# Sample cross-attention with stationary queries in quarter tiles, and state space parameters worked out during the input projection

## The chip, the cores and the metric

The kernel runs on one core of one Trainium2 chip. The metric is device time in microseconds (us) of one execution, from launch to end, as the median of several runs. The core has five engines with queues of their own: TensorE (PE, with its weight loads listed apart as PEld), VectorE (DVE), ScalarE (ACT), GpSimd (POOL) and SyncE (SP, which only issues transfers). An engine takes its instructions strictly in the order of its queue; engines wait for each other by semaphores.

## What is computed

One inference step of one decoder layer, for a prompt of 1024 tokens and, with the same weights, for 64 sample tokens (8 sequences of 8 tokens with a paged cache of 8192 past tokens each). Cut to the parts that the change touches:

```python
z = rmsnorm(x, norm_mix_pre) @ w_in          # one projection: 1024 -> 1056 columns
c_q, c_kv, k_r, u = split(z)                 # 256 | 256 | 32 | 512
attn_out = mla_mixer(c_q, c_kv, k_r, ...)    # samples: attention over the paged cache
# state space mixer: 32 groups x 16 channels, 64 states
dt  = exp(ssm_log_dt); mag = exp(dt * a_re)
abr, abi = mag * cos(dt * a_im), mag * sin(dt * a_im)
...                                          # powers of (abr, abi), input and output tables, scan, GLU
# cross-attention of 4 heads x 128 into 256 memory tokens; for the samples mk, mv are caches per sequence
q  = (h @ w_q_mem).reshape(b, l, 4, 128)
s  = einsum('bqhd,bmhd->bhqm', q, mk) * MEM_SCALE
pr = softmax(s)
o  = einsum('bhqm,bmhd->bqhd', pr, mv).reshape(b, l, 512) @ w_o_mem
# then a gated MLP of 2816 columns
```

## The kernel before, in words

The layer is a chain of stages. In the profiled execution they lie as follows: projection 0 to 129 us (`stage_in`), paged sample attention with everything that is put beside it 129 to about 700 (`stage_par`), prompt attention to 873, mixing to 991, cross-attention to 1204 (`stage_mem`), the MLP to the end.

**Projection.** Nine tiles of tokens: the 64 samples first (numbered 8), then prompt tiles t = 0 to 7. Each takes 72 matmuls of up to 512 columns into three PSUM banks `z` (L488), split into high and low halves for three-product accuracy: ACT makes `xh` from `xT`, DVE `xl` (L325, L326), one tile ahead. A tile's `z` is read out by ACT (`cz`) and by DVE (`kr_raw` L496, two copies into `u_all` L498 and L499). At t == 2 `dec_start` prepares the sample queries of the paged attention: they go through DRAM, `qld` and then `Qb` in four transfers of 512 KB on SP, and POOL issues the gathers of the first cache pages `kf` and `rf`.

**The parallel stage.** `gen_dec` walks the cache: DVE transposes each gathered block (`kT<-kf`, L1033, eight blocks of 1.2 us, and one of `rf`), PE makes scores S (L1044), DVE their maxima (`mx`, L1065), ACT exponentials, PE transposes and values (`ov`, L1109). Beside it a generator `side()` runs `gen_ssm`, `gen_glu`, `gen_memkv`, `gen_q` and `gen_attw`. The instructions of both are recorded and put into a new order by a class `Order` (list scheduling by costs, for PE, DVE, ACT and POOL); SP's transfers keep their place by the recorded order and priorities. `gen_ssm` begins with a parameter part: it loads `prm` (L617), computes two exponentials by polynomials on DVE (L634 to L645), phases with a Sin table on ACT (L669, L670), powers `pw` by squaring on DVE and POOL, factors `f` and tables `cs`. It also brings the sample inputs `u_sn` as `us8`, 8 partitions, in 8 transfers (L623), and turns them by 32 PE transposes of 8x8 blocks (L736) into `Us`. Then come tables and chunks per state group (`BB`, `W1T`, `W`, scan `Z`).

**Cross-attention.** `stage_mem` runs prompt tiles t = 0 to 7 of 128 tokens: query transposes, `project(t - 1)` (output projection, L1736), scores and softmax (L335 to L337, L1751 to L1758), the next tile's query projection `query_z`, transposes of the probabilities `Pm` (L1839) and values (L1850). The sample work is put among the tiles by a hand-written list `sample[t]`. Scores: `sample_k(b)` keeps the keys of a sequence stationary (128x128 per head and half of the memory) and moves the 8 query columns (L1777), 8 matmuls for each of 8 sequences, t = 1 to 4. At t = 5 `sample_w` and `sample_pT` transpose all scores (64 rows x 4 heads), make the softmax, and transpose back. Values: `sample_v(b)` keeps V stationary and moves 8 columns of the transposed probabilities (L1809), t = 5 and 6. `sample_o` is the output projection of the samples at t = 7. PSUM: six banks `b` for the prompt, one bank `sbank` and one bank `smp` for the samples. Each f32 matmul is two passes in the trace, so L1777 and L1809 have 128 passes each; a transpose is one.

Of the kernel before, what the change touches and what calls it, by code (L numbers as in the profile page):

```python
# [9 lines left out]
F32 = mybir.dt.float32  # L10
# [3 lines left out]
AF = mybir.ActivationFunctionType  # L14
OP = mybir.AluOpType
AX = mybir.AxisListType
# [282 lines left out]
class Kern:  # L299
# [96 lines left out]
    def stage_in(self):  # L396
# [82 lines left out]
        for n, t in enumerate(order):  # L479
# [40 lines left out]
            if t == 1:  # L520

                qctx = ExitStack()
                qp = self.pool("q_s", 1, qctx, side="right")
                w = self.q_weights(qp, qp)
                self.q_s = pers.tile([64, 768], F32, tag="qy", name="q_s")
                self.query_rows(qp, [zp.tile([128, 512], F32, tag="z", name="z") for _ in range(2)], self.q_s,
                                self.cqTh_s, self.cqTl_s, *w, self.csS[:, 0], self.csS[:, 1])
                qctx.close()
            if t == 2:
                self.dec_start(lambda: zp.tile([128, 512], F32, tag="z", name="z"))  # L530
# [72 lines left out]
    def gen_ssm(self):  # L603
# [44 lines left out]
        exp(w["dt"][:, None, :], ldt[:, None, :], 1)  # L648
        ex = new(c2, "ex", [128, 2, 32])
# [3 lines left out]
        exp(mags, ex, 2)  # L653
        rho8 = new(c1, "rho8", [128, 32])
# [17 lines left out]
        V.tensor_scalar(ph[:, 0], s2, -2.0, 1.0, op0=OP.mult, op1=OP.add)  # L672

# [7 lines left out]
        for n in (1, 2, 4):  # L681
            bc = lambda a: a[:, None, :].to_broadcast([128, n, 32])
            self.cmul([pw[:, k, n + 1:2 * n + 1] for k in (0, 1)], [pw[:, k, 1:n + 1] for k in (0, 1)],
                      [bc(pw[:, k, n]) for k in (0, 1)], [t[:, :n] for t in tmp], V, G)
        pwr = pw[:, :, 7::-1]
# [17 lines left out]
        V.tensor_scalar_mul(f[:, 3], w["t2"], -1.0)  # L703

# [23 lines left out]
        ssd = new(c1, "ssd", [16, 32])  # L728
        nc.sync.dma_start(ssd, i["ssm_d"])

        pp = self.pool("sp", 2, ctx, space=PSUM)
        psum = lambda: pp.tile([128, 512], F32, tag="ps", name="ps")
        Us = new(c1, "Us", [128, 32, 8])
        ps = psum()[:, 0:256].rearrange("p (g b) -> p g b", b=8)
        for g in range(32):
            nc.tensor.transpose(ps[:, g], us8[:, g].rearrange("p j c -> p (j c)"), self.ident[:8, :8])  # L736
        nc.scalar.activation(Us, ps, AF.Copy)
        tctx.close()
# [945 lines left out]
    def stage_mem(self):  # L1684
# [17 lines left out]
        kv = lambda: sp.tile([128, 2, 512], F32, tag="kv", name="kv")  # L1702
# [57 lines left out]

        smp = {}

        def sample_q(q):
            ps = sbank()
            for h in range(4):
                nc.tensor.transpose(ps[:, h, :64], q[:, h * 128:(h + 1) * 128], self.ident[:64, :64])
            smp["qT"] = sp.tile([128, 4, 64], F32, tag="qTs", name="qTs", bufs=1)
            V.tensor_copy(smp["qT"], ps[:, :, :64])
            smp["st"] = ps_.tile([128, 2, 4, 64], F32, tag="smp", name="smp")

        def sample_k(b):
            qT, st = smp["qT"], smp["st"]
            kT = flat(kv()).rearrange("p (h k m) -> p h k m", h=4, k=2)
            nc.sync.dma_start(kT.rearrange("p h k m -> p (h k m)"), i["mem_kT"][b])
            for k in range(2):
# [4 lines left out]
        def sample_w():  # L1780
            sT = sp.tile([128, 2, 4, 64], F32, tag="sT", name="sT", bufs=1)
            V.tensor_copy(sT, smp["st"])
            ps = sbank()
            s4 = ps.rearrange("p (a k) m -> p a (k m)", a=2)
            for a in range(2):
                for k in range(2):
                    nc.tensor.transpose(ps[:, a * 2 + k], sT[:, k, 2 * a:2 * a + 2].rearrange("p h t -> p (h t)"),
                                        self.ident)
            Pm = smp["P"] = sp.tile([128, 2, 256], F32, tag="Pms", name="Pms", bufs=1)
            l = sp.tile([128, 4], F32, tag="l8", name="l8")  # L1790
            softmax(s4, 2, Pm, l, 0, "mx8")

        def sample_pT():
            Pm = smp["P"]
            ps = sbank()
            for a in range(2):
                for k in range(2):
                    nc.tensor.transpose(ps[:, k * 2 + a], Pm[:, a, k * 128:(k + 1) * 128], self.ident)
            smp["pT"] = sp.tile([128, 2, 4, 64], F32, tag="sT", name="pTs", bufs=1)
            V.tensor_copy(smp["pT"].rearrange("p k h t -> p (k h t)"), flat(ps))  # L1800
            smp["po"] = ps_.tile([128, 2, 4, 64], F32, tag="smp", name="smp")[:, 0]

        def sample_v(b):
            pT, po = smp["pT"], smp["po"]
            vb = kv()
            nc.sync.dma_start(vb, i["mem_v"][b].rearrange("(k p) d -> p k d", p=128))
            for h in range(4):
                for k in range(2):
                    nc.tensor.matmul(po[:, h, b * 8:(b + 1) * 8], vb[:, k, h * 128:(h + 1) * 128],  # L1809
                                     pT[:, k, h, b * 8:(b + 1) * 8], start=k == 0, stop=k == 1)  # L1810

        def sample_o():
            oh = lp.tile([128, 4, 128], F32R, tag="oh", name="oh")
            ol = lp.tile([128, 4, 128], F32R, tag="ol", name="ol")
            self.split(oh[:, :, :64], ol[:, :, :64], smp["po"])
            project(8, oh, ol)
# [42 lines left out]
        for k in range(4):  # L1859
# [3 lines left out]
        two = lambda f, b: [lambda: f(b), lambda: f(b + 1)]  # L1863
# [347 lines left out]
```

## Time and profile before

| | |
|---|---|
| median of 3 runs | 2007.9 us (2007.51 to 2022.9) |
| profiled execution, its own time | 2011.3 us |
| its span, first to last instruction | 2009.5 us |
| busy: PE | 1875.4 us, 93% |
| busy: DVE, ACT, POOL | 1099.2, 802.3, 515.9 us (55, 40, 26%) |
| mean granted clock of TensorE | 0.955 of full speed |
| chain that ended last, by engine | PE 74%, DVE 8%, DMA 6%, issue 5%, ACT 4% |

Busy shares are means over stages with different limits. The tables by stretch show which engine is full where, and what clock TensorE was granted there (1.00 is 2.4 GHz, half of it 1.2 GHz). In a timeline a row is a run of equal instructions; the bracket at its end is the engine's idle time before it and what ended that. For PE, a row's time holds the pipeline's tail, so the price of one pass is better read from one row's start to the next row's.

### The profile page before, as it was taken

The numbers are of one execution on the slowest core, as the hardware profiler recorded it, in microseconds if no ns is written. First come the engines' busy times: TensorE is split into PE (matmuls) and PEld (weight loads), VectorE is DVE, ScalarE is ACT, GpSimd is POOL, SyncE is SP. The second block draws the span as 40 slices with busy tenths as digits, with TensorE's granted clock in tenths as the row PEclk, the third lists the DMA queues.
The fourth block names the chain that finished last, engine by engine and source line by source line (L and its number), as shares of the span: only waits on it lengthen the run. The fifth ranks groups of instructions, "written<-read, shape, count | busy, mean of one in ns | idle before, by whom it ended". The sixth has DMA issues, their size and how long they took to land.

```text
span 2009.5 us, 32068 instructions
## 1 busy us (share of the span) xinstructions
PE 1875.4 (93%) x12747; PEld 1486.4 (74%) x12747; DVE 1099.2 (55%) x2000; ACT 802.3 (40%) x1578; POOL 515.9 (26%) x549
## 2 busy tenths in 40 slices
PE   8967799789898899999999989999999999999997
PEld 6853455355454588777788978888888999999776
DVE  4238999775556588843334464443545533334333
ACT  5312233143332378853333344333444333333332
POOL 1312111131121033325301022222144421110554
PEclk9988889899899999999979999999999999999999
DMA  7713534455477511141123453223333522222221
GB/s 245 234 41 123 198 129 146 143 207 190 156 255 265 151 55 40 64 147 38 66 92 99 148 179 121 93 86 105 94 114 108 170 85 85 81 78 88 74 80 62
DMA packets 136550, 247.94 MB, mean 123 GB/s; under 512 B 26897, under 2 KB 91217, under 8 KB 132305
## 3 DMA queue, kind: packets, MB, share of 16 engines
q1 hardware_dynamic: 129072, 169.87, 27.0%
q0 software_dynamic: 7328, 76.03, 9.9%
q8 instruction: 100, 1.64, 0.3%
q14 instruction: 50, 0.40, 0.1%
HBM read 217.13 MB, written 27.29 MB: 122 GB/s over the span
## 4 chain that ended last, share of the span: by engine, by line
PE 74%; DVE 8%; DMA 6%; issue 5%; ACT 4%; POOL 1%; SPq 1%; DVEq 0%; ACTq 0%; POOLq 0%
PE ps L2069 26%; PE z L1581 5%; PE ps L335 4%; PE ps L337 4%; PE ps L336 4%; PE z L488 4%; PE S L1044 3%; PE ov L1109 3%; DVE kT L1033 2%; PE b L1736 2%; DMA kf<-in_cache_kv_dram,idx 2%; PE t L1384 1%; DMA W<-ky 1%; PE b L335 1%; PE b L336 1%
## 5 line engine op out<-in xcount | busy, mean ns | idle before, releaser
L2069 PE MATMUL ps<-xTl,wh 128*128 128x288 f32 (+1 forms) x1056 | 288.4, 327 | 0.0
L2069 PE MATMUL ps<-xTh,wh 128*128 128x288 f32 (+1 forms) x1056 | 288.2, 327 | 0.0
L2069 PE MATMUL ps<-xTh,wl 128*128 128x288 f32 (+1 forms) x1056 | 288.2, 327 | 0.0
L326 POOL TENSOR_TENSOR wl<-st,wh 128x1024 fp32r<-128x1024 f32 (+1 forms) x52 | 115.8, 2227 | 410.9 <-ACT wh L325 410.9
L1044 PE MATMUL S<-kT,Qb 32*64 32x512 f32 x2304 | 161.6, 663 | 39.2 <-DVE kT L1033 18.0
L326 DVE TENSOR_TENSOR wl<-st,wh 128x1024 fp32r<-128x1024 f32 (+1 forms) x52 | 62.1, 1195 | 246.0 <-ACT wh L325 246.0
L325 ACT ACTIVATE wh<-st 128x1024 fp32r<-128x1024 f32 (+1 forms) x104 | 102.5, 994 | 234.2 <-PE ps L2069 212.5
L2069 PEld LDWEIGHTS ps<-xTh,wh 128*128 128x128 f32 x1056 | 180.1, 189 | 14.1
L2069 PEld LDWEIGHTS ps<-xTl,wh 128*128 128x128 f32 x1056 | 180.0, 189 | 13.8
L2069 PEld LDWEIGHTS ps<-xTh,wl 128*128 128x128 f32 x1056 | 179.9, 189 | 13.9
L326 DVE TENSOR_TENSOR wdl<-std,wdh 128x1024 fp32r<-128x1024 f32 x44 | 100.3, 2282 | 147.3 <-ACT wdh L325 147.3
L1033 DVE STREAM_TRANSPOSE kT<-kf 128x1024 f32<-128x1024 f32 x128 | 151.6, 1220 | 25.2 <-DMA kf<-in_cache_kv_dram,idx 17.5
L2020 POOL TENSOR_TENSOR al<-act,ah 128x1024 fp32r<-128x1024 f32 x44 | 106.8, 2426 | 174.0 <-ACT ah L2019 174.0
L335 PE MATMUL ps<-wdh,ah 128*128 128x512 f32 x352 | 139.5, 396 | 0.0
L336 PE MATMUL ps<-wdl,ah 128*128 128x512 f32 x352 | 139.1, 395 | 0.0
L1109 PE MATMUL ov<-kf,PT 128*64 128x256 f32 x1024 | 128.7, 399 | 0.6 <-ACT PT L1094 0.6
L337 PE MATMUL ps<-wdh,al 128*128 128x512 f32 x352 | 126.1, 396 | 0.0
L1044 PEld LDWEIGHTS S<-kT,Qb 32*64 32x64 f32 x2304 | 44.2, 142 | 98.5 <-issue 41.2
L1109 PEld LDWEIGHTS ov<-kf,PT 128*64 128x64 f32 x1024 | 71.3, 142 | 52.1 <-issue 18.1
L2019 ACT ACTIVATE ah<-act 128x1024 fp32r<-128x1024 f32 (+1 forms) x44 | 49.0, 1113 | 142.2 <-PE ps L336 141.4
L335 PEld LDWEIGHTS ps<-wdh,ah 128*128 128x128 f32 x352 | 66.2, 188 | 17.4 <-issue 0.8
L337 PEld LDWEIGHTS ps<-wdh,al 128*128 128x128 f32 x352 | 66.1, 188 | 15.6
(532 smaller groups left out, 3972.9 us busy)
## 6 DMA issues: line engine op xcount, KB each, us to landing
st<-in_w_gate_dram SPq DMA_DIRECT2D x22, 1024.0 KB
st<-in_w_up_dram SPq DMA_DIRECT2D x22, 1024.0 KB
std<-in_w_down_dram SPq DMA_DIRECT2D x44, 512.0 KB
x<-in_x_prompt_dram SPq DMA_DIRECT2D x16, 512.0 KB
x<-x2d SPq DMA_DIRECT2D x15, 512.0 KB
wst<-in_w_in_dram SPq DMA_DIRECT2D x8, 528.0 KB
xT<-in_xT_dram SPq DMA_DIRECT2D x8, 512.0 KB
ws<-in_w_out_dram SPq DMA_DIRECT2D x8, 512.0 KB
```

Of the source, the lines that this page charges most:

```text
L325: nc.scalar.activation(hi, src, AF.Copy)
L326: (lo_eng or nc.vector).tensor_sub(lo, src, hi.bitcast(F32))
L335: mm(ps, lh, rh, start=start, stop=False)
L336: mm(ps, lh, rl, start=False, stop=False)
L337: mm(ps, ll, rh, start=False, stop=stop)
L488: nc.tensor.matmul(z[:P, :c1 - c0], lhs[:, k, :P], rhs[:, k, c0:c1], start=a, stop=b)
L1033: V.transpose(t, RF[n] if kb == 8 else KF[n][:, :, :, kb * 32:kb * 32 + 32])
L1044: nc.tensor.matmul(SS[n][half[a], j], Qb[q, kb, 2 * p + a], ts[q, a], start=kb == BLOCKS[0], stop=kb == BLOCKS[-1])
L1109: nc.tensor.matmul(ov[half[a]], PTS[n, g][:, m, half[a]], KF[n][:, a, g * 4 + m], start=g == 0 and m == 0, stop=g == 3 and m == 3)
L1581: nc.tensor.matmul(z[n], l, r[:, n * 512:(n + 1) * 512], start=a, stop=b)
L2020: G.tensor_sub(al, a[:, :, :512], ah[:, :, :512].bitcast(F32))
L2069: nc.tensor.matmul(zt[:, :c1 - c0], l[:, k], r[:, k, c0:c1], start=a, stop=b)
```

## The change

**One: the state space parameters move.** `gen_ssm` takes a function `bank` and becomes a generator that is started at projection tile t = 2 and advanced twice in each of the tiles 3 to 7; the remainder runs in `stage_par` as before. The sample inputs go from `u_sn` to a DRAM buffer `usd` (8 transfers), come back as one tile `us` of 32 partitions x 1024 (in the buffer of `wide`, so that its load follows the last reader of `wide`), and are turned by 8 transposes of 128x32 in a `z` bank of the projection, instead of 32 transposes of 8x8 blocks in a bank of their own.

**Two: the operands of the sample cross-attention change places.** For a pair p of sequences, `sample_s(p)` keeps 32 columns of queries stationary and moves the 256 memory columns of the keys; the four heads write to four partition quarters of one bank. The softmax is made straight on that layout (128 partitions x 2 x 256), without transposes before it. `sample_v(p)` transposes the probabilities (4 transposes of 128x128), keeps 32 of their columns stationary and moves the 128 columns of V per head, divides by the sum while ACT copies the result, transposes it back (2 transposes) and copies it to `oT`. The `kv` buffers become 3 instead of 2. The pairs are put at t = 1 to 5.

```diff
             if t == 2:
-                self.dec_start(lambda: zp.tile([128, 512], F32, tag="z", name="z"))
+                self.dec_start(zbank)
+                self.ssm_groups, opened = self.gen_ssm(zbank), False
+            if 2 < t < 8:
+                for _ in range(2):
+                    opened = opened or next(self.ssm_groups)
...
-    def gen_ssm(self):
+    def gen_ssm(self, bank):
...
-        us8 = new(c2, "us8", [8, 32, 8, 16])
+        usd = self.pool("usd", 1, space=DRAM).tile([8, 32, 8, 16], F32, name="usd")
         for j in range(8):
-            nc.sync.dma_start(us8[:, :, j], self.u_sn.rearrange("(b j) (g c) -> j b g c", j=8, c=16)[j])
+            nc.sync.dma_start(usd[:, :, j], self.u_sn.rearrange("(b j) (g c) -> j b g c", j=8, c=16)[j])
...
+        us = new(c2, "us", [32, 1024], "wide")
+        nc.sync.dma_start(us, usd.rearrange("b (q g) j c -> (b q) (g j c)", q=4))
+        yield
...
-        for g in range(32):
-            nc.tensor.transpose(ps[:, g], us8[:, g].rearrange("p j c -> p (j c)"), self.ident[:8, :8])
...
+        for g in range(8):
+            nc.tensor.transpose(ps[:, g], us[:, g * 128:(g + 1) * 128], self.ident[:32, :32])
...
-            yield from self.gen_ssm()
+            yield from self.ssm_groups
...
-                    nc.tensor.matmul(st[:, k, h, b * 8:(b + 1) * 8], kT[:, h, k], qT[:, h, b * 8:(b + 1) * 8],
-                                     start=True, stop=True)
...
+                    nc.tensor.matmul(s[quarter(h), j], smp["qT"][:, h, b * 8:b * 8 + 32], kT[:, h], start=True, stop=True)
+            mx = sp.tile([128, 2], F32, tag="mx8", name="mx8")
+            V.reduce_max(mx, s, axis=AX.X)
+            V.tensor_scalar_mul(mx, mx, -MSC)
...
+            for j in range(2):
+                nc.scalar.activation(Pm[:, j], s[:, j], AF.Exp, bias=mx[:, j:j + 1], scale=MSC, accum_out=l[:, j:j + 1])
...
+            pT = sp.tile([128, 4, 128], F32, tag="pTs", name="pTs", bufs=1)
+            V.tensor_copy(pT, ps)
...
-                    nc.tensor.matmul(po[:, h, b * 8:(b + 1) * 8], vb[:, k, h * 128:(h + 1) * 128],
-                                     pT[:, k, h, b * 8:(b + 1) * 8], start=k == 0, stop=k == 1)
+                        nc.tensor.matmul(po[quarter(h), j], pT[:, j * 2 + k, quarter(h)], vb[:, k, h * 128:(h + 1) * 128],
+                                         start=k == 0, stop=k == 1)
+                nc.scalar.activation(o[:, j], po[:, j], AF.Copy, scale=l[:, j:j + 1])
             ps = sbank()
+            for j in range(2):
+                nc.tensor.transpose(ps[:, j], o[:, j], self.ident)
...
-        sample = [[], two(sample_k, 0), two(sample_k, 2), two(sample_k, 4), two(sample_k, 6),
-                  [sample_w, sample_pT] + two(sample_v, 0) + two(sample_v, 2),
-                  two(sample_v, 4) + two(sample_v, 6), [sample_o]]
+        sample = [[], [piece(sample_s, 0)], [piece(sample_v, 0), piece(sample_s, 1)], [piece(sample_v, 1), piece(sample_s, 2)],
+                  [piece(sample_v, 2), piece(sample_s, 3)], [piece(sample_v, 3)], [], [sample_o]]
```

**Where instructions now stand.** First, SP's queue during projection tiles 3 to 5. Before:

```order
L971 DMA Qb<-qld 32x8x512 x4
L729 DMA ssd<-in_ssm_d_dram 16x32
L422 DMA xT<-in_xT_dram 128x1024
L514 DMA out_dram<-cn 128x256
L515 DMA lat<-cn 128x512
L422 DMA xT<-in_xT_dram 128x1024
```

And of the change:

```order
L987 DMA Qb<-qld 32x8x512 x4
L625 DMA prm<-in_ssm_par_dram 128x128
L633 DMA ssd<-in_ssm_d_dram 16x32
L422 DMA xT<-in_xT_dram 128x1024
L514 DMA out_dram<-cn 128x256
L515 DMA lat<-cn 128x512
L686 DMA us<-usd 32x1024
L422 DMA xT<-in_xT_dram 128x1024
```

The load of the parameters `prm` now stands right behind `Qb`, and the load of `us` ahead of the last tile's `xT`; before, `prm` and the sample inputs came after the last row of the projection. The `usd` stores stand earlier, among the loads of the first tiles.

DVE's queue at the read-out of projection tile 3 (`rs_595` is that tile's factor). Before:

```order
L678 MEMSET pw 128x32
L496 TENSOR_SCALAR kr_raw<-z,rs_595 128x32
L498 TENSOR_SCALAR u_all<-z,rs_595 128x15x16
L499 TENSOR_SCALAR u_all<-z,rs_595 128x17x16
L326 TENSOR_TENSOR xl<-xT,xh 128x512 x2
L509 SCALAR_TENSOR_TENSOR cn<-cz,rs_886,b_kv_norm 128x256
```

And of the change, where 18 more of the same exponential's instructions stand ahead, the first of them `nsgn<-prm`:

```order
L619 TENSOR_TENSOR ey<-ey,er 128x32
L654 TENSOR_SCALAR ey<-ey 128x32
L496 TENSOR_SCALAR kr_raw<-z,rs_595 128x32
L498 TENSOR_SCALAR u_all<-z,rs_595 128x15x16
L499 TENSOR_SCALAR u_all<-z,rs_595 128x17x16
L619 TENSOR_TENSOR ey<-ey,er 128x32
L326 TENSOR_TENSOR xl<-xT,xh 128x512 x2
```

The read-out of tile 3 and the split `xl` for tile 5 now stand behind instructions that read `prm`. The next pieces stand in the same way ahead of the read-outs of tiles 4 and 5; tiles 6 and 7 have none.

Second, DVE's queue where the parallel stage's first block of pages is transposed (`kT<-kf`). Before, the parameter part's last instructions stand ahead of it:

```order
L600 TENSOR_TENSOR pw<-pt_1508 128x128
L611 TENSOR_TENSOR pt_1508<-cs_1553,ph 128x64
L706 COPY p_1549<-pw 128x32
L1033 STREAM_TRANSPOSE kT<-kf 128x1024 x8
L611 TENSOR_TENSOR pt_1509<-cs_1553,ph 128x64
L611 TENSOR_TENSOR p_1549<-pw,prm 128x32
L1033 STREAM_TRANSPOSE kT<-rf 128x1024
L1065 TENSOR_REDUCE mx<-S 128x1
```

And of the change:

```order
L619 TENSOR_TENSOR A_1899<-ps,csn 64x4x128 x2
L619 TENSOR_TENSOR big_1931<-BB,pw 128x4x128
L619 TENSOR_TENSOR A_1900<-A_1898,A_1899 128x4x128
L619 TENSOR_TENSOR W1T<-W1T,big_1931 128x512
L884 SCALAR_TENSOR_TENSOR Z<-rho_1111,A_1900 128x128 x4
L1049 STREAM_TRANSPOSE kT<-kf 128x1024 x8
L1049 STREAM_TRANSPOSE kT<-rf 128x1024
L619 TENSOR_TENSOR A_1953<-Z,csn 64x4x128 x2
L1081 TENSOR_REDUCE mx<-S 128x1
```

The tables of the first state groups and the scan `Z` of the first chunk, which before stood behind the second block of pages, now stand ahead of the first.

Third, PE's queue in cross-attention around the sample work of tile 2 (of tile 1 in before, where `sample_k` stands). Before:

```order
L1839 MATMUL b<-ident,Pm 128x128 x2
L1777 MATMUL smp<-qTs,kv 128x8 x2
L1839 MATMUL b<-ident,Pm 128x128 x4
L1777 MATMUL smp<-qTs,kv 128x8 x2
L1850 MATMUL b<-pT,mv 128x128
L1709 MATMUL b<-ident,x_9468 128x128 x8
L1709 MATMUL b<-ident,q 128x128 x4
L1777 MATMUL smp<-qTs,kv 128x8 x3
L1850 MATMUL b<-pT,mv 128x128 x7
L1777 MATMUL smp<-qTs,kv 128x8 x13
```

And of the change (`Pms`, `pTs`, `os` are the sample pair's probabilities, their transpose and its output):

```order
L1817 MATMUL b<-ident,Pms 128x128 x4
L1827 MATMUL smp<-kv,pTs 32x128 x8
L1863 MATMUL b<-ident,Pm 128x128 x8
L1827 MATMUL smp<-kv,pTs 32x128 x8
L1832 MATMUL b<-ident,os 128x128
L1874 MATMUL b<-pT,mv 128x128
L1725 MATMUL b<-ident,x_9448 128x128 x8
L1725 MATMUL b<-ident,q 128x128 x4
L1874 MATMUL b<-pT,mv 128x128 x7
L1832 MATMUL b<-ident,os 128x128
L1800 MATMUL b<-kv,qTs 32x256 x8
```

The transposes of `Pms` stand directly ahead of the values that need their copy, and the transposes of `os` ahead of the next pair's scores (L1800), with prompt work between some of them.

## Rows read from the trace of the kernel before

**Rows 1.** The page's head: span and instructions.

```profile
span 2009.5 us, 32068 instructions
```

**Rows 2.** Table by stretch, parallel stage: stretch, length, busy times, PEclk, DMA share, GB/s.

```profile
129.00:155.00 26.00, 5.41 (x52) 4.07 (x52) 19.53 (x104) 3.80 (x9) 6.47 (x19) 0.55 0.13 34
...
182.00:260.00 78.00, 66.21 (x626) 37.75 (x632) 72.10 (x158) 25.69 (x72) 10.43 (x13) 0.87 0.41 141
260.00:400.00 140.00, 121.19 (x1300) 66.88 (x1292) 127.40 (x257) 43.18 (x121) 23.56 (x22) 0.89 0.40 146
400.00:550.00 150.00, 135.12 (x1275) 79.15 (x1260) 96.78 (x137) 57.80 (x131) 39.10 (x37) 0.92 0.50 185
```

**Rows 3.** Table by stretch, cross-attention: busy of PE, PEld, DVE, ACT, POOL; then PEclk.

```profile
1012.00:1070.00 58.00, 57.62 (x307) 53.41 (x308) 18.84 (x38) 17.13 (x41) 4.91 (x11) 0.74 0.32 101
1070.00:1100.00 30.00, 29.17 (x160) 24.64 (x159) 14.93 (x36) 12.14 (x36) 4.13 (x10) 1.00 0.19 70
1100.00:1157.00 57.00, 57.00 (x363) 51.99 (x362) 26.91 (x47) 20.45 (x48) 5.84 (x14) 0.91 0.43 144
```

**Rows 4.** Lines L1777 and L1809: passes, duration min/median/max in ns, first and last start.

```profile
L1777 PE MATMUL smp<-qTs,kv x128: 170/256/361, 1013.3 to 1068.5; 128*128 128x8 f32 x128
...
L1809 PE MATMUL smp<-pTs,kv x128: 170/256/362, 1100.8 to 1155.7; 128*128 128x8 f32 x128
```

**Rows 5.** Timeline of PE: start, length, line, tiles, stationary size, moving size, passes.

```profile
190.58 0.41 PE L825 MATMUL ps<-W,BB 128*16 128x128 f32 x8
190.92 1.30 PE L1109 MATMUL ov<-kf,PT 128*64 128x256 f32 x10
...
267.23 3.69 PE L1044 MATMUL S<-kT,Qb 32*64 32x512 f32 x64
270.85 1.16 PE L854 MATMUL ps<-U,W 128*128 128x128 f32 x8
...
1056.17 1.84 PE L1777 MATMUL smp<-qTs,kv 128*128 128x8 f32 x16
1057.88 1.07 PE L1839 MATMUL b<-ident,Pm 128*128 128x128 f32 x8
...
1127.55 1.73 PE L1850 MATMUL b<-pT,mv 128*128 128x128 f32 x14
1129.11 3.34 PE L1809 MATMUL smp<-pTs,kv 128*128 128x8 f32 x26
```

**Rows 6.** Timeline of cross-attention: DVE and ACT, the sample softmax of before.

```profile
1081.88 0.69 DVE L1751 TENSOR_REDUCE mx<-b 128x2 f32<-128x512 f32 x1 [0.60 <-PE b L1787]
...
1083.88 0.47 ACT L1754 ACTIVATE Pms<-b,mx 128x256 f32<-128x256 f32 x1 [0.64 <-DVE mx L1752]
```

**Rows 7.** Timeline of SP, DVE and ACT during projection tiles 4 and 5.

```profile
81.40 1.80 SPq L971 DMA_DIRECT2D Qb<-qld  x4
...
84.81 0.35 SPq L422 DMA_DIRECT2D xT<-in_xT_dram  x1
...
94.07 0.25 DVE L496 TENSOR_SCALAR kr_raw<-z,rs 128x32 f32<-128x32 f32 x1 [6.84 <-PE z L488]
...
95.73 1.15 ACT L325 ACTIVATE xh<-xT 128x512 fp32r<-128x512 f32 x2 [8.47 <-DMA xT<-in_xT_dram]
```

**Rows 8.** Timeline of DVE and PE at the start of the parallel stage.

```profile
132.59 0.18 DVE L634 TENSOR_SCALAR ek<-prm 128x32 f32<-128x32 f32 x1 [0.66 <-DMA prm<-in_ssm_par_dram]
...
153.72 9.12 DVE L1033 STREAM_TRANSPOSE kT<-kf 128x1024 f32<-128x1024 f32 x8
...
155.01 9.00 PE L1044 MATMUL S<-kT,Qb 32*64 32x512 f32 x128 [12.68 <-DVE kT L1033]
...
181.70 0.17 DVE L819 TENSOR_TENSOR kd<-ident,ssd 16x64 f32<-16x64 f32 x1
...
209.80 0.42 DVE L1118 COPY O<-ov 128x256 f32<-128x256 f32 x1
...
215.37 0.69 DVE L611 TENSOR_TENSOR W1T<-BB,pw 128x512 f32<-128x512 f32 x1
```

More of the change, by code (lines that the diff above doesn't have):

```diff
@@ L528, in stage_in @@
                 qctx.close()
+            zbank = lambda: zp.tile([128, 512], F32, tag="z", name="z")
             if t == 2:
-                self.dec_start(lambda: zp.tile([128, 512], F32, tag="z", name="z"))
+                self.dec_start(zbank)
[3 more added lines that the diff above has]
+                    opened = opened or next(self.ssm_groups)
+        while not opened:
+            opened = next(self.ssm_groups)
         nc.sync.dma_start(o["kr_p"].rearrange("(c j) r -> c j r", j=8), kr_rot)
@@ L653, in gen_ssm @@
         exp(mags, ex, 2)
+        yield
         rho8 = new(c1, "rho8", [128, 32])
@@ L703, in gen_ssm @@
         V.tensor_scalar_mul(f[:, 3], w["t2"], -1.0)
+        yield
         p8 = new(c1, "p8", [128, 2, 32])
@@ L1701, in stage_mem @@
         flat = lambda a: a.rearrange("p a n -> p (a n)")
-        kv = lambda: sp.tile([128, 2, 512], F32, tag="kv", name="kv")
+        kv = lambda: sp.tile([128, 2, 512], F32, tag="kv", name="kv", bufs=3)
         def transposed(xh, xl, x):
@@ L1783, in sample_w, with sample_v @@
+        def sample_v(p):
+            Pm, l = smp.pop(p)
             ps = sbank()
-            s4 = ps.rearrange("p (a k) m -> p a (k m)", a=2)
-            for a in range(2):
+            for j in range(2):
                 for k in range(2):
-                    nc.tensor.transpose(ps[:, a * 2 + k], sT[:, k, 2 * a:2 * a + 2].rearrange("p h t -> p (h t)"),
-                                        self.ident)
-            Pm = smp["P"] = sp.tile([128, 2, 256], F32, tag="Pms", name="Pms", bufs=1)
@@ L1790, in sample_w @@
[L1790 to L1794, printed above, removed]
-            ps = sbank()
[L1796 to L1808, printed above, removed]
-                    nc.tensor.matmul(po[:, h, b * 8:(b + 1) * 8], vb[:, k, h * 128:(h + 1) * 128],
-                                     pT[:, k, h, b * 8:(b + 1) * 8], start=k == 0, stop=k == 1)
+                    nc.tensor.transpose(ps[:, j * 2 + k], Pm[:, j, k * 128:(k + 1) * 128], self.ident)
@@ new lines, in sample_v @@
+            pT = sp.tile([128, 4, 128], F32, tag="pTs", name="pTs", bufs=1)
+            V.tensor_copy(pT, ps)
+            po = ps_.tile([128, 2, 128], F32, tag="smp", name="smp")
+            o = sp.tile([128, 2, 128], F32, tag="os", name="os", bufs=1)
+            for j in range(2):
+                vb = kv()
+                nc.sync.dma_start(vb, i["mem_v"][2 * p + j].rearrange("(k p) d -> p k d", p=128))
+                for k in range(2):
+                    for h in range(4):
+                        nc.tensor.matmul(po[quarter(h), j], pT[:, j * 2 + k, quarter(h)], vb[:, k, h * 128:(h + 1) * 128],
+                                         start=k == 0, stop=k == 1)
+                nc.scalar.activation(o[:, j], po[:, j], AF.Copy, scale=l[:, j:j + 1])
@@ L1812, in sample_o @@
+            ps = sbank()
+            for j in range(2):
+                nc.tensor.transpose(ps[:, j], o[:, j], self.ident)
+            V.tensor_copy(smp["oT"].rearrange("p h (b q) -> p b h q", q=8)[:, 2 * p:2 * p + 2],
+                          ps[:, 0:2].rearrange("p b (h q) -> p b h q", q=32)[:, :, :, 0:8])
         def sample_o():
@@ L1814, in sample_o @@
             ol = lp.tile([128, 4, 128], F32R, tag="ol", name="ol")
-            self.split(oh[:, :, :64], ol[:, :, :64], smp["po"])
+            self.split(oh[:, :, :64], ol[:, :, :64], smp["oT"])
             project(8, oh, ol)
```

43 lines of the change are left out of this document (25 added, 18 removed).

## The prediction

> **What bounds the kernel now.** I read the page's head and the shares first: PE is busy for 93% of a span of 2009.5 us [rows 1], so a gain must come from less PE work, a faster TensorE clock, or one of the few places where PE waits. The tables by stretch show two such places. At the start of the parallel stage PE does 5.41 us of work in 26 us while DVE is busy for 19.53; from 260 to 400 us DVE is still the fuller engine, 127.40 of 140 us against PE's 121.19, and after 400 PE leads, 135.12 of 150 [rows 2]. So time saved on DVE at the start is not swallowed at once: DVE passes it on until 400, PE after that. In cross-attention PE is never idle for long (57.62 of 58 us, 57.00 of 57), but its granted clock is 0.74 in the stretch with the sample scores and 0.91 in the one with the sample values, against 1.00 between them, where there is no sample pass [rows 3, 4]. That is 58 x 0.26 + 57 x 0.09 = 20 us lost to the lower of the two levels (1.2 instead of 2.4 GHz). DVE and ACT are under half busy there.
>
> **Cross-attention, work.** Removed are 256 passes [rows 4]. At full clock 16 of them take 1.71 us from start to next start [rows 5], 0.107 each though only 8 columns move, and 14 passes that move 128 columns take 1.56, 0.111 each: a pass of before is paid by its 128-column weight load, not by its 8 columns. 256 x 0.107 = 27.4 us; 8 transposes at 0.111 add 0.9. Gone: 28.3.
>
> Added are 64 score passes (8 sequences x 4 heads x 2) of 256 columns and 128 value passes of 128 columns, each on 32 stationary columns. The trace of before has no such shape, so I bound it. The nearest row for the scores is the paged S, a quarter-height, half-width tile with 512 columns: 64 passes in 3.62 us, 0.057 each [rows 5], the same area times columns as here; 64 x 0.057 = 3.6. The nearest for the values is a 16-column tile moving 128 columns: 8 passes in 0.34 us, 0.043 each [rows 5], 128 x 0.043 = 5.4. Both are below what an unshared pass would take (0.111 for 128 columns, so 0.222 for 256), so tiles do run beside each other. If the quarters did not, scores and values would be 14.2 us each. I take the low ends, 9.0 together. 24 transposes at 0.111 are 2.7.
>
> The 16-column row also holds the way into and out of the tile shape, since full-width transposes precede it and half-width values follow. The Trainium skill, TensorEngine Tiling (Array Packing), Key Properties, says that a change of tiling mode drains TensorE, which speaks against some 12 blocks and twice as many changes; this case's row agrees with no large cost, since both changes fit in its 0.34 us. By the rule alone the sum would only grow by an unknown drain.
>
> New waits: values stand right behind the transposes whose copy they need, and the next scores behind a copy out of the one sample bank. A DVE read of a whole bank is 0.69 us [rows 6]. I take 1 us for each of the four pairs, 4 us; nothing at the least, since prompt passes stand between some of them, and the rival below at the most. Behind the waiting instruction on PE stands only prompt work that DVE and ACT feed from their spare half. The key loads have three buffers and a tile's time ahead of them; I cost them at nothing, and if that cover were gone, one load would show as a PE wait on `kv`. The softmax has the same shape as before, four times instead of once: 4 x (0.69 + 2 x 0.47) us [rows 6], on engines under half busy. Work and waits: -28.3 + 9.0 + 2.7 + 4 = -12.6 us.
>
> **Cross-attention, clock.** The lower clock lies where 8-column passes lie [rows 3, 4]. With those gone I expect most of the 20 us back, but not all, since the short tiles come with transposes and small pauses. I take 12, between 0 and 20. Sum of this part: **-25 us**, between -12.6 and -37.
>
> **Parameters, what leaves the parallel stage.** DVE works through them from 132.59 to 153.72 us [rows 8], 21.1 us until the first page block is transposed, and PE waits 12.68 us for that. About 1 us more of `cs` tables follows later. All of it, 22 us, moves under the projection, where DVE mostly waits for PE, 6.84 us ahead of the read-out of tile 4 [rows 7]. The 32 small transposes and the late sample loads go too; they lie beside DVE work and I cost them at nothing.
>
> **What the projection pays.** DVE takes its queue in order, and the read-out of tile 3 and the split for tile 5 now stand behind a wait for `prm`. On SP `prm` stands right behind `Qb`, four transfers issued at 81.40; the `xT` behind these, issued at 84.81, is only used at 95.73 [rows 7]. So `prm` should land at about 93 to 95. Then come some 20 instructions of about 0.12 us, the read-out and the split: tile 5, which before began at about 94, begins at about 98. Late next: the read-out of tile 4, behind the Sin table and the load of `us`, some 2 us more at tile 6; and a pause may lower the clock for some 5 us, another 2 to 3. Sum +8 us: the projection's last matmul at about 137 instead of 128.7. Bounds: +2, if `prm` passes `Qb` on other engines of the transfer system, and +22, if nothing is won.
>
> **What that makes of the parallel stage.** The order now puts tables and the first scan, some 23 us of DVE work (before within 181.70 to 209.80), ahead of the first page block [rows 8]. So the block's transposes come at about 137 + 26 = 163, later than the 153.72 of before, and only behind them does the gain show. Before, it took from 153.72 to 215.37 to reach what in the new order is done when the first `O` is copied; without those 23 us that is 163 + 61.7 - 23 = 201.7. Gain 14 us, the same as 22 - 8. DVE and then PE carry it to the end of the stage [rows 2]. **-14 us**, between 0 and -20.
>
> **Sum.** 2011.3 (the profiled execution's own time) - 25 - 14 = 1972. It lies 3.4 above the median of the runs shown, so I predict 1970 for the median.
>
> **Rivals.** (a) *The clock does not come back*: the sample blocks remain short and broken up. For it: it also dropped before without idle time in PE. Against: between the two sample stretches the same prompt work ran at 1.00. The stage saves 12.6: 2011 - 12.6 - 14 = 1985, 1981 as median. The Trainium skill, TensorE: Matmul & The Clock Gate, Part 4, says that transposes don't count for the clock as other passes do; there are 24 here for 8 of before, and by that rule this rival is the result; no row here separates it. (b) *The projection pays all back*: the wait for `prm` plus half-clock stretches cost 22 us. For it: three tiles' read-outs stand behind SSM work. Against: DVE has some 4 to 7 us to spare in each tile. Then only cross-attention gains: 1986, 1983 as median. (c) *The quarters do not run side by side*: scores and values 28.4 instead of 9.0, so the part saves 5.6: 1992, 1988 as median. Against: the two rows of small tiles. (d) *The other side*: each pair is a chain through one bank (scores, maximum 0.69, two exponentials, transposes, copy 0.7, values, copies, transposes, copy), some 5.5 us if PE stands through all of it, 22 for four pairs, and each pause lowers the clock over some 10 us, 20 more, with the old 20 not won back: -16.6 + 42 - 14 = +11, 2022, 2019 as median. It decides once a pair costs over (16.6 + 14) / 4 = 7.6 us. Against: prompt passes stand between most steps.
>
> **Chances.** Forecast 0.48, its own range 1956 to 1977; (a) 0.20, (b) 0.18, (c) 0.08, (d) 0.06. The range 1948 to 1992 takes in (a) to (c) and, at its low end, all of the clock with no waits and -20 in the parallel stage (2008 - 37 - 20 = 1951). This kernel's runs tell about 1% from no change, 20 us. Faster by over 1% (below 1988): the forecast, (a) and most of (b), 0.83. Within 1%: (c), the rest of (b), most of (d), 0.13. Slower: 0.04.
>
> **What would show it.** In the new profile: PEclk of the sample tiles above 0.9 (else a); score passes near 0.06 and value passes near 0.04 us from start to start (else c); PE idle ahead of the sample's transposes and values under 1 us per pair (else d); a PE wait of about 4 us near 94 us and the projection's end near 137 (else b, or more gain); first page block at about 163, first `O` copied near 202. The prediction is wrong if the parallel stage does not pass the gain on, or if the stage's length falls by less than 12 us.

## The result: somewhat over half of the forecast, and none of it shown to come from the first part

| | before | after |
|---|---|---|
| median, 7 runs each | 2013.64 us (2007.51 to 2022.9) | 1993.59 us (1987.95 to 1998.42) |
| ratio to before, 95% interval | 1 | 0.989 (0.9865 to 0.9915) |
| span of the profiled execution | 2009.5 us | 1986.1 us |

The change makes the kernel 1.1% faster: 0.011 x 2010 = 22 us, 17 to 27 by the interval. Forecast were 38 (a ratio of 0.981, outside the interval). The forecast's own range, 1956 to 1977 us, is 0.974 to 0.985 of the median it was worked out from and does not hold the result; the wide range, 0.970 to 0.992, does, because it took in the rivals. Later comparisons had other medians for the kernel before, so everything below goes by ratios within one comparison.

The profile by stages (tables by stretch, cut at the first or last matmul of a stage; columns as in [rows 2]). Before, projection, parallel stage and cross-attention:

```profile
0.00:128.50 128.50, 116.65 (x722) 102.53 (x723) 41.31 (x83) 50.98 (x102) 30.51 (x90) 0.97 0.62 197
128.50:697.30 568.80, 482.09 (x4838) 276.82 (x4837) 426.04 (x841) 184.25 (x453) 103.06 (x112) 0.90 0.48 173
...
991.40:1203.80 212.40, 201.19 (x1133) 174.92 (x1133) 100.76 (x183) 89.34 (x210) 31.40 (x69) 0.89 0.39 127
```

After, the same:

```profile
0.00:140.20 140.20, 120.62 (x730) 106.27 (x731) 59.05 (x190) 53.82 (x106) 37.06 (x99) 0.94 0.58 183
140.20:700.30 560.10, 482.44 (x4806) 276.13 (x4805) 412.66 (x734) 181.97 (x449) 95.04 (x103) 0.92 0.49 175
...
996.50:1181.70 185.20, 169.41 (x1086) 136.28 (x1085) 105.97 (x197) 93.81 (x230) 30.82 (x70) 0.98 0.43 146
```

Cross-attention is 27 us shorter here, at a clock of 0.98 instead of 0.89. The parallel stage is 9 us shorter, but the projection ends 12 later, so the stage ends at 700 instead of 697. The forecast's 14 us of the first part are not there.

**Cross-attention after**, the stretches with sample work, to be read beside [rows 3]:

```profile
1017.00:1066.00 49.00, 44.37 (x299) 36.04 (x292) 23.55 (x51) 21.66 (x61) 5.53 (x14) 0.97 0.34 119
1066.00:1100.00 34.00, 33.40 (x246) 27.59 (x245) 20.65 (x43) 16.32 (x44) 4.35 (x10) 1.00 0.45 157
1100.00:1140.00 40.00, 39.74 (x265) 33.14 (x264) 23.88 (x51) 17.73 (x50) 3.84 (x11) 1.00 0.36 130
```

And PE's timeline there, the score and value passes with the row behind each, to be read beside [rows 5]:

```profile
1030.15 0.65 PE L1827 MATMUL smp<-kv,pTs 128*32 128x128 f32 x16 [0.78 <-DVE pTs L1819]
...
1056.42 0.64 PE L1827 MATMUL smp<-kv,pTs 128*32 128x128 f32 x16
1057.00 0.73 PE L1752 MATMUL b<-woh,oh 128*128 128x512 f32 x2
...
1075.32 1.07 PE L1800 MATMUL b<-kv,qTs 128*32 128x256 f32 x16
1076.33 0.73 PE L1752 MATMUL b<-woh,oh 128*128 128x512 f32 x2
```

A score pass costs (1076.33 - 1075.32) / 16 = 0.063 us, a value pass (1057.00 - 1056.42) / 16 = 0.036; forecast were 0.057 and 0.043. The 192 passes are 64 x 0.063 + 128 x 0.036 = 8.6 us, against 9.0 forecast, and the waits that the new blocks show are 0.3 to 0.8 us each.

**The projection and the start of the parallel stage after**, to be read beside [rows 7] and [rows 8]. SP, DVE and PE in the projection:

```profile
66.82 4.07 PE L981 MATMUL z<-qnT,wukT 64*128 64x64 f32 x29 [4.82 <-DVE qnT L971]
...
81.56 0.65 SPq L625 DMA_DIRECT2D prm<-in_ssm_par_dram  x1
...
92.00 0.15 DVE L627 TENSOR_SCALAR nsgn<-prm 128x1 f32<-128x1 f32 x1 [19.85 <-DMA prm<-in_ssm_par_dram]
...
95.10 0.25 DVE L496 TENSOR_SCALAR kr_raw<-z,rs 128x32 f32<-128x32 f32 x1
...
117.96 0.24 DVE L496 TENSOR_SCALAR kr_raw<-z,rs 128x32 f32<-128x32 f32 x1
...
108.16 0.68 PE L749 MATMUL z<-ident,us 32*128 32x32 f32 x8
...
112.09 0.51 PE L488 MATMUL z<-winh,xh 128*128 128x512 f32 x2
118.73 0.57 PE L488 MATMUL z<-winh,xh 128*128 128x272 f32 x1 [6.13 <-DVE u_all L498]
```

DVE stands still for 19.85 us for `prm`, then works with hardly a pause, and is late for the read-out of tile 5 at 117.96; PE waits 6.13 us for that bank, in the middle of tile 6: the row before the wait has two matmuls where a full step has three (`x2`), the third group's bank being not yet free. Then DVE and PE at the start of the parallel stage:

```profile
149.07 2.02 PE L1060 MATMUL S<-kT,Qb 32*64 32x512 f32 x16 [7.25 <-DVE kT L1049]
...
163.43 1.36 DVE L884 TENSOR_TENSOR_SCAN Z<-rho,A 128x128 f32<-128x128 f32 x4
164.71 9.10 DVE L1049 STREAM_TRANSPOSE kT<-kf 128x1024 f32<-128x1024 f32 x8
...
165.98 9.55 PE L1060 MATMUL S<-kT,Qb 32*64 32x512 f32 x128 [3.73 <-DVE kT L1049]
...
200.08 0.42 DVE L1134 COPY O<-ov 128x256 f32<-128x256 f32 x1 [0.57 <-PE ov L1125]
```

The first block of pages is transposed at 164.71 (forecast 163) and the first `O` copied at 200.08 (forecast 202). These two came out; what I had taken them to mean did not.

### The profile page after: what moved, and what is told of

Read it like the earlier page. It is cut to its first block, busy times and chain, and to the rows that moved or that the text cites. A ratio compares the mean times of both kernels' runs of the same rounds, so it can differ in the third digit from the quotient of the medians.

```text
span 1986.1 us, 31961 instructions
## 1 busy us (share of the span) xinstructions
PE 1846.4 (93%) x12675; PEld 1450.1 (73%) x12675; DVE 1109.6 (56%) x2013; ACT 807.4 (41%) x1598; POOL 514.4 (26%) x550
## 4 chain that ended last, share of the span: by engine, by line
PE 62%; ACT 2%; DVE 2%; issue 1%; POOL 1%; DMA 1%; SPq 0%; DVEq 0%; ACTq 0%; POOLq 0%
PE ps L2092 26%; PE z L1597 5%; PE ps L335 4%; PE ps L337 4%; PE ps L336 4%; PE b L1752 2%; PE t L1400 1%; PE S L1060 1%; PE ov L1125 1%; PE o L1416 1%; PE o L1417 1%; PE s L1378 1%; PE s L1379 1%; PE s L1380 1%; PE b L335 1%
## 5 line engine op out<-in xcount | busy, mean ns | idle before, releaser
L2092 PEld LDWEIGHTS ps<-xTh,wh 128*128 128x128 f32 x1056 | 179.6, 188 | 13.7
L335 PE MATMUL ps<-wdh,ah 128*128 128x512 f32 x352 | 139.5, 396 | 0.0
L1027 POOL DMA_INDIRECT kf<-in_cache_kv_dram,idx x32 | 33.3, 1040 | 175.1 <-PE ov L1125 169.3
```

Of the source, the lines that this page charges most:

```text
L335: mm(ps, lh, rh, start=start, stop=False)
L2092: nc.tensor.matmul(zt[:, :c1 - c0], l[:, k], r[:, k, c0:c1], start=a, stop=b)
```

## Experiments

All are compared with the kernel before on the same chip. Beside the ratio the table gives, from each profile: the end of the projection, the length of the parallel stage (to the last value matmul of its end), the third maximum `mx` on DVE (the paged attention's third of 16 blocks), what remains of the stage from there, and mixing and cross-attention together. Times in us.

| kernel | projection ends | stage | third `mx` at | rest of stage | mix + cross | ratio (95%) |
|---|---|---|---|---|---|---|
| before | 128.5 | 568.8 | 239.9 | 457.4 | 330.5 | 1 |
| changed | 140.2 | 560.1 | 235.0 | 465.3 | 306.1 | 0.989 (0.9865, 0.9915) |
| e1: first part alone | 139.7 | 552.6 | 233.5 | 458.8 | 327.5 | 0.9998 (0.9975, 1.0021) |
| e2: second part alone | 129.1 | 571.4 | 246.1 | 454.4 | 307.5 | 0.9922 (0.990, 0.9944) |
| e3: changed, `prm` early | 130.9 | 554.9 | 225.8 | 460.0 | 306.4 | 0.9827 (0.9803, 0.9851) |
| e4: changed, pages known | 140.1 | 536.8 | 226.0 | 450.9 | 305.4 | 0.9813 (0.9788, 0.9838) |
| e5: e3 and e4 | 132.3 | 537.8 | 217.3 | 452.8 | 305.7 | 0.9767 (0.9737, 0.9797) |
| e6: before, pages known | 130.5 | 569.7 | 245.1 | 455.1 | 322.7 | 0.9996 (0.9972, 1.002) |
| e7: second part, pages known | 126.9 | 569.1 | 240.6 | 455.5 | 306.7 | 0.9931 (0.9911, 0.9951) |
| c1: changed, matmul price | 140.7 | 563.5 | 235.7 | 468.5 | 307.0 | 0.9883 (0.9846, 0.992) |
| c2: changed, DVE price | 139.5 | 554.3 | 238.2 | 455.6 | 309.8 | 0.9813 (0.9776, 0.9849) |
| c3: e4, matmul price | 141.8 | 559.9 | 229.6 | 472.1 | 306.3 | 0.9842 (0.9803, 0.9881) |
| c4: e4, DVE price | 140.4 | 535.0 | 224.9 | 450.5 | 301.1 | 0.9763 (0.9727, 0.9799) |
| e8: e5, DVE price | 130.3 | 531.7 | 215.6 | 446.4 | 305.8 | 0.9661 (0.9625, 0.9697) |

**Which part gave the 22 us?** The kernel e1 is the changed one with `stage_mem` of before; e2 is the kernel before with the new `stage_mem`.

> Only the first part of the change: the state space parameters and sample inputs among the projection's tiles, cross-attention as before. The forecast's theory (a lead of 14 us is passed on to the end): 14 us faster, ratio 0.993. The rival (the projection gives up as much as the parallel stage wins, and the replanned stage keeps no lead): 0 to 3 us slower, ratio 1.000 to 1.002, with the projection ending near 140 us and the last value matmul of the paged attention near 700 instead of 697.

> Only the second part: the sample cross-attention with stationary queries, the rest as before. Both theories: 24 us faster, ratio 0.988, granted clock of the stage near 0.98 instead of 0.90. If instead the forecast's 25 us were a chance sum of another split (say 12 here and 12 elsewhere), the ratio would be near 0.994.

The first part alone is worth nothing: 0.9998, known to 0.23% either way. The second part alone gives 0.9922, 16 us (11 to 20), less than the 24 that I had expected under both theories, at a clock of 0.96; and the changed kernel differs from e1 by 0.011, 22 us. By the profiles, mixing and cross-attention take 322.7 to 330.5 us in the three kernels with the old order of operands and 301.1 to 309.8 in the eleven with the new one, about 21 us less. So the gain of the second part is shown and none of the first. From e2 to the changed kernel there are 6 us more (0.9922 to 0.989), but the intervals overlap, so that is not shown to be a gain. The forecast lost its first part whole, or all but a few us of it.

**Does the projection eat it?** In the changed kernel the projection ends 11.7 us later. In e3 one transfer is moved:

```diff
-        nc.sync.dma_start(prm, i["ssm_par"])
+        with self.tc.high_priority(2000):
+            nc.sync.dma_start(prm, i["ssm_par"])
```

> The changed kernel with one transfer moved: the parameter load stands ahead of the four large Qb transfers on SP, so that DVE need not wait for it until 92 us; the planned order of the parallel stage is the same. If the projection's loss is what ate the gain and the stage passes a start on unchanged: the projection ends at 131 to 133 instead of 140, the parallel stage ends 7 to 9 us earlier, ratio to the kernel before 0.985. If the parallel stage is paced by something that an earlier start does not move: the projection ends earlier but the ratio stays at 0.989.

SP and DVE in e3, where `prm` is issued before `Qb`:

```profile
72.67 0.33 SPq L626 DMA_DIRECT2D prm<-in_ssm_par_dram  x1
80.55 1.81 SPq L988 DMA_DIRECT2D Qb<-qld  x4
...
80.73 0.15 DVE L628 TENSOR_SCALAR nsgn<-prm 128x1 f32<-128x1 f32 x1 [8.77 <-DMA prm<-in_ssm_par_dram]
...
89.11 0.25 DVE L496 TENSOR_SCALAR kr_raw<-z,rs 128x32 f32<-128x32 f32 x1
```

DVE has `prm` 11 us earlier, PE no longer waits at tile 6, the projection ends at 130.9, the third `mx` comes 9.2 us earlier, and the ratio falls to 0.9827, 13 us better than the changed kernel (intervals of 0.25% on each). The stage passes an earlier start on. So the loss in the projection was real and was paid in full at the end. (The stage's end comes 14.5 us earlier; the 5 beyond the 9.2 lie behind the third `mx`, within what the same order of instructions varies by between executions, as shown below.)

**And the rest?** With the projection nearly at its old end, e3 is 19 us better than e2 (0.9922 to 0.9827). I suspected a second loss in it all the same. In the changed kernel, and in e3 in the same way, DVE's order puts tables and a scan ahead of the first page block, as the order ahead of the prediction showed. That order comes from a planner that treats the first page gathers as issued at the start of the parallel stage; in the trace they are issued at about 60 us. The edit of e4 corrects that one belief:

```diff
+        for k in [k for k, x in enumerate(tr) if type(x).__name__ == "InstDMACopy" and eng[k] == "Pool"][:4]:
+            work[k] = (10.0, 20.0) + work[k][2:]
         prio, best = list(range(n)), None
```

> The changed kernel, with one number of the planner changed: it takes the first four page gathers as landed (the trace shows them issued at about 60 us, long before the parallel stage). The first page block is then transposed right behind the projection, about 143 us instead of 165, and the tables come among the blocks. If the gain is lost because the paged attention's first block stands behind the tables: the stage ends 10 to 20 us earlier, ratio 0.980 to 0.984. If the stage is held by its total work or by the ring of page gathers whatever stands first: within 4 us of the changed kernel, ratio 0.987 to 0.991.

DVE in e4, and the first 25 us of the stage in the changed kernel and in e4:

```profile
143.56 1.23 DVE L1051 STREAM_TRANSPOSE kT<-rf 128x1024 f32<-128x1024 f32 x1
144.72 2.32 DVE L1051 STREAM_TRANSPOSE kT<-kf 128x1024 f32<-128x1024 f32 x2
...
186.11 0.37 DVE L1136 COPY O<-ov 128x256 f32<-128x256 f32 x1
```

```profile
140.20:165.00 24.80, 13.30 (x99) 9.87 (x97) 19.77 (x53) 6.04 (x17) 8.39 (x15) 0.57 0.65 226
```

```profile
140.10:165.00 24.90, 17.87 (x211) 10.56 (x209) 21.60 (x40) 7.10 (x18) 8.75 (x16) 0.79 0.72 252
```

(The first of the two rows is the changed kernel, the second e4.) PE gets scores to do at once: 211 passes instead of 99, at a clock of 0.79 instead of 0.57. The first `O` is copied at 186 instead of 200, the stage is 23 us shorter, and the ratio is 0.9813, 15 us better than the changed kernel. Together with the early `prm` (e5), and as a control in the kernel before (e6) and in the one with the second part alone (e7):

> The changed kernel with both edits of the runs before: parameter load ahead of Qb, and the planner taking the first page gathers as landed. If the two losses are separate (projection 9 us, first block behind the tables 16 us), they add: ratio to the kernel before 0.968 to 0.974. If both are one loss seen twice (the time at which the first block's transposes begin): no more than the better of the two, 0.978 to 0.982.

> The kernel before, with the planner taking the first page gathers as landed and nothing else. If the wrong belief was harmless before, because the parameter part filled that time: within 5 us, ratio 0.997 to 1.000. If it cost the kernel before as much as the changed one: 16 us faster, ratio 0.992, and then it is a fault that both have and not where the change lost its gain.

> The second part of the change (cross-attention) and the planner taking the first page gathers as landed, with the parameter part in the parallel stage as before. Against e5 this is the value of moving the parameter part once neither the wait for prm nor the planner's belief takes it back. By the forecast's count (22 us of DVE work, little paid by the projection) e5 is 14 to 20 us faster than this run; if work moved off DVE is not what the stage is short of, e5 and this run agree within 5 us.

The two edits nearly add: 0.9767, between the two ranges that I had given, where the sum of both gains would be 0.975. The same belief was harmless before: 0.9996 in e6, and e7 agrees with e2. In e6 DVE does transpose the first block at once, and then is held by the parameter part, which still lies ahead of all tables:

```profile
135.01 2.33 DVE L1035 STREAM_TRANSPOSE kT<-kf 128x1024 f32<-128x1024 f32 x2
...
149.22 2.29 DVE L1067 TENSOR_REDUCE mx<-S 128x1 f32<-128x2048 f32 x1 [1.03 <-PE S L1046]
...
212.56 2.27 DVE L1067 TENSOR_REDUCE mx<-S 128x1 f32<-128x2048 f32 x1
```

The first maximum comes 15 us earlier than before, the second 21 us later, the third at 245. With the parameters in place the order moved nothing: from the projection's end to the third `mx` DVE is busy for 96 to 100 us and idle for 14 to 21 in all four kernels, the block ahead (e6, e7) or behind (before, e2). With the parameters gone that is no longer so, and the order counts. Once both losses are taken away, moving the parameters is worth e7 against e5: 0.9931 to 0.9767, 33 us, with intervals of 0.2 and 0.3%. That is beyond the 14 to 20 that I expected of this pair, and more than the work that was moved. The stretch from the projection's end to the third `mx`, e7 and then e5 (busy times of PE, PEld, DVE), shows most of it:

```profile
126.90:240.60 113.70, 81.25 (x826) 47.18 (x824) 100.01 (x271) 28.73 (x76) 21.04 (x34) 0.80 0.39 140
```

```profile
132.30:217.30 85.00, 70.92 (x782) 38.69 (x780) 82.17 (x161) 25.77 (x70) 22.55 (x25) 0.88 0.49 172
```

DVE has 17.8 us less to do, and is idle for 2.8 instead of 13.7 us. The stretch is 28.7 us shorter, and as it begins 5.4 later, the third `mx` comes 23 earlier. Of the other 8 us between the two profiles' spans (1988.6 and 1957.1), 5 lie in prompt attention (179.4 and 174.7 us).

**Is it the place of the first block, or the luck of a plan?** A list scheduler gives another order for any change of its prices. Four controls change a price and leave the place of the first block as it was, behind the tables (c1, c2) or ahead of them (c3, c4). In c1 and c3:

```diff
-            return 1.1 * t, 1.1 * t + 250.0
+            return 1.15 * t, 1.15 * t + 250.0
```

In c2 and c4:

```diff
-            t = 120 + 1.1 * n
+            t = 125 + 1.12 * n
```

> A control for the luck of a plan: the changed kernel, with the planner's price of every matmul raised by 5% (1.15 instead of 1.1), which gives another order with the same place for the first page block, behind the tables. If what the pages edit won came from that place: as the changed kernel, parallel stage 552 to 562 us, ratio 0.987 to 0.992. If any new plan may win or lose that much: the stage differs by over 10 us from 556.

> A second control: the changed kernel, with the planner's price of DVE work raised by 2 to 4%, another order with the first page block still behind the tables. Place theory: parallel stage 552 to 562 us, ratio 0.987 to 0.992. Luck theory: it differs by over 10 us from 556.

> The pages edit (first gathers taken as landed) together with the matmul price of the first control. Place theory: parallel stage 533 to 541 us as with the pages edit alone, ratio 0.978 to 0.984. Luck theory: it may as well lie at 550 or more.

> The pages edit together with the DVE price of the second control. Place theory: parallel stage 533 to 541 us, ratio 0.978 to 0.984. Luck theory: it may as well lie at 550 or more.

For the length of the stage c2 and c4 came as the place theory said: 554.3 behind the tables, 535.0 ahead of them; c1, at 563.5, lies 1.5 beyond the range, but not the 10 of the luck theory. c3 did not: first block ahead, and yet 559.9. The column of the third `mx` tells the two apart. With the projection ending at about 140 it comes at 235.0, 235.7 and 238.2 with the block behind the tables (changed, c1, c2), and at 226.0, 229.6 and 224.9 with it ahead (e4, c3, c4): 9, 6 and 13 us earlier in the three pairs, 9 on average. DVE's rows for that stretch say why. Changed and e4, c1 and c3, c2 and c4:

```profile
140.20:235.00 94.80, 72.16 (x762) 37.90 (x761) 82.59 (x161) 23.84 (x65) 16.89 (x24) 0.82 0.40 139
```

```profile
140.10:226.00 85.90, 73.00 (x782) 39.35 (x780) 82.27 (x161) 25.58 (x69) 22.99 (x26) 0.84 0.47 163
```

```profile
140.70:235.70 95.00, 73.62 (x756) 38.32 (x755) 82.32 (x161) 22.83 (x61) 17.27 (x25) 0.80 0.39 136
```

```profile
141.80:229.60 87.80, 74.25 (x782) 39.55 (x780) 82.44 (x163) 25.61 (x70) 21.31 (x25) 0.84 0.47 162
```

```profile
139.50:238.20 98.70, 77.22 (x782) 40.35 (x780) 85.53 (x165) 25.57 (x68) 17.96 (x26) 0.78 0.41 147
```

```profile
140.40:224.90 84.50, 72.35 (x792) 40.12 (x791) 82.30 (x162) 27.15 (x73) 20.18 (x26) 0.88 0.51 181
```

DVE's work is nearly the same, 82 to 86 us. It is idle for 12 to 13 us where the block stands behind the tables, and for 2 to 5 where it stands ahead, c3 among them. So the place of the first block is worth what DVE no longer waits. The rest of the stage is a matter of the plan: 450.5 to 472.1 us in these six. Kernels whose DVE and ACT have the same order of instructions in the stage agree there to 6.5 us at most (before 457.4 and e2 454.4; e6 455.1 and e7 455.5; changed 465.3, e1 458.8, e3 460.0; e4 450.9, e5 452.8; c4 450.5, e8 446.4). So of the 23 us by which e4's stage is shorter, 9 are the place of the first block, and 14 lie in the rest (some 10 by the means of the kernels with the same order), which c3 shows need not come with it. c2's ratio of 0.9813 lies outside what I had given, and the profiles do not explain it: its stage ends 6.5 us earlier than the changed kernel's by a shorter rest, but the spans of the two profiles differ by 1 us (1985.0 and 1986.1), c2's being the slowest of its four runs and the other the fastest of seven. The ratios of c3 and c4, 0.9842 and 0.9763, lie a little outside what I had given, on either side.

**All that helped, together** (`prm` early, pages known, DVE price):

> The changed kernel with the parameter load ahead of Qb, the first gathers taken as landed, and the planner's DVE price of the second control: the sum of what helped. If the projection's 9 us and the place of the first block are separate gains in this plan too: projection end near 132, parallel stage 533 to 538 us, ratio 0.968 to 0.976. If the second is a matter of one lucky plan: stage 545 us or more, ratio 0.979 or above.

0.9661, a little better than the range: 68 us faster than before and 46 faster than the changed kernel. The projection ends at 130.3, the third `mx` is there at 215.6, and the rest takes 446.4, the shortest of all.

## Why the prediction was right, and where it was wrong

**Right: the sign, and cross-attention's mechanism.** The result lies within the wide range, and that is partly luck: it is where rival (b) was put (a ratio of 0.988), with one part short and the other lost. By the sign that the prediction set itself, that it is wrong if the parallel stage does not pass the gain on, its first part is wrong. For the second part: a pass of before was paid by its weight load, and the quarters run beside each other: 8.6 us for scores and values against 9.0. The waits were some 5 us (PE idle there is 15.8 us after and 11.2 before: 185.20 - 169.41 and 212.40 - 201.19), against 4. Rivals (a), (c) and (d) fall: the clock is 0.97 to 1.00 in the stretches with sample work, the passes cost what the small tiles said, no pair stalls for long. The transposes did not hold the clock down. The Trainium skill, TensorE: Matmul & The Clock Gate, Part 4, which says that they don't count as other passes do, had stood for rival (a); with 24 sample transposes in it the stage ran at 0.98, so what the page says does not decide here.

**Mis-sized: its clock.** The part was to give 25 us and gave 13 (e7 against e6), 16 (e2) and 22 (changed against e1); by the intervals one gain of 15 to 19 would fit all three. In the profile that I worked from, cross-attention ran at 0.89; in e1 and e6, with the same code, at 0.92, and 6 us shorter. I had read the size of a clock loss from one execution. With the new order of operands the stage ran at 0.94 to 0.99 in the eleven profiles. The term was 12 us; from 0.92 to about 0.97 over some 200 us it is 10, and less of it in those kernels where the new stage ran at 0.95. That explains a few us. The profiles show the stages themselves about 21 us shorter; why the medians of two of the three pairs show less was not settled.

**Wrong: "what the projection pays", +8.** It was 11.7. The arrival of `prm` was right (92.00 us; I had said 93 to 95), but not where PE would stop. There is no wait near 94: six `z` banks let PE run on while DVE is late by one tile. From 92 to 119 us DVE has work with hardly a pause, and PE stops at tile 6, 6.13 us instead of 2, with half-clock rows behind it (0.23 us from one pass of 272 columns to the next, 0.12 in the same rows of e3). It stops there for the read-out of tile 5, not of tile 4, which the prediction named. A tile takes three of the six banks, so tile 6 would have had those that tile 5 left over, had not the eight transposes of `us` (L749, at 108.16) taken one of them. The prediction gave these transposes no price. What the bank alone cost was not tried. Another 2.4 us I had not seen at all: PE's wait for `qnT` at 66 us grew to 4.82 from what PE's timeline of before has:

```profile
65.08 2.83 PE L965 MATMUL z<-qnT,wukT 64*128 64x64 f32 x29 [2.47 <-DVE qnT L955]
```

In the trace ACT waits 3.84 us for the last tile's `x`, whose load SP issues at 58.42 instead of 52.73 with the eight `usd` stores ahead of it; the split `xh`, and on DVE `xl` and `qnT`, stand behind that wait. What the stores alone cost was not tried.

**Wrong: "what that makes of the parallel stage", -14.** Two things in that step. First, 22 us of DVE work were to leave; DVE's busy time in the projection grew from 41.3 to 59.05 us, so 17.7 came in there, and 13.4 left the parallel stage (426.04 to 412.66). The stretch that I had read as 21.1 us of work, 132.59 to 153.72, holds 17.02 us of DVE work, 1.24 of it the page block `rf`, and waits. Second, and larger, I set the state at the first `O` of the new order equal to the state at 215.37 of the old one. The time was right (200.08) and the equation was not: DVE had tables and scans in hand, but the paged attention was behind, its second maximum at 207 instead of 191. By the third the lead was 5 us, 7 on average over the runs (235.6 in the four kernels with the parameters moved, the block behind the tables and the projection ending near 140, 242.9 in four with the parameters in place). I should have compared the chain that goes on, blocks of pages that each need the buffer of an earlier one, and not the sum of work done. And then the new plan took 6 us longer for the rest than the old one (461.4 in changed, e1 and e3, 455.6 in before, e2, e6 and e7). In sum the stage became 14 us shorter (555.9 on average in the one group, 569.8 in the other) where 22 were forecast, and the projection took back 11.7 where 8 were: 2 are left, and e1 shows none. Rival (b), at 0.18, was right in its outcome, though it named the projection alone.

**What stays open.** Why the plans differ by up to 20 us after the third block, at equal work (PE 405 to 410 us busy, DVE 326 to 330, in the stretch after the third maximum in before, changed and e4), was not settled; their waits are spread over many small ones. Of the 33 us that moving the parameters is worth in e5, 17.8 us of DVE work and 10.9 of its waits ahead of the third maximum, less the projection's 5.4, are accounted for; why those waits stay with the parameters in place, whatever the order (e6, e7), is not shown, nor where all of the rest lies.

## What to carry to other kernels

Where a matmul moves few columns past a large stationary block, put the small operand into the weights and use quarter tiles: price both by rows of the same kernel with small tiles, and take the clock from several executions. When early work is moved out of a stage whose order a planner sets, look up what the planner puts into the place, and what it believes about transfers that were issued before the stage; a wrong belief that cost nothing as long as other work covered it can take the gain. When work is put into an idle engine's queue ahead of read-outs that another engine needs, the first operand's arrival decides: load it ahead of the large transfers of its queue.

## What the runs showed that I had not expected

One load of 64 KB, issued at 81.56 us behind four transfers of 512 KB on the same queue, was usable at 92.00; issued before them at 72.67, at 80.73, and this alone was worth 13 us (0.989 to 0.9827). A change of 2 to 4% in a planner's price of DVE work was followed by about as much (c2 against the changed kernel, 0.9813 to 0.989), without the profiles showing where.
